# Cross attention's values by seven block products with sums made in DRAM, weight splits on VectorE alone, output products by heads, in a one-core fp32 decoder layer

## The chip, the cores and the metric

The kernel runs on one core of a Trainium2 chip. The metric is the time of one execution in device microseconds (us); a version is judged by the median of several runs. A profile records one more execution; its own time stands beside its span, since the span starts with the first recorded instruction. Engines in the rows: PE is TensorE, PEld its weight load, DVE is VectorE, ACT is ScalarE, POOL is GpSimd, SP is SyncE, which here only issues DMAs. A name with a q (SPq, POOLq) is the engine's sequencer.

## What is computed

One layer of a decoder in fp32, 256 tokens of width 1024, with 256 memory tokens. The part that the change touches is cross attention (4 heads of 256) and its surroundings:

```python
def memory_cross_attention(h, mem, wq, wkv, wo):
    q = (h @ wq).reshape(B, S, X_HEADS, X_HEAD_DIM)
    kv = mem @ wkv
    k = kv[..., :D_MODEL].reshape(B, M, X_HEADS, X_HEAD_DIM)
    v = kv[..., D_MODEL:].reshape(B, M, X_HEADS, X_HEAD_DIM)
    s = jnp.einsum('bshd,bmhd->bhsm', q, k).astype(jnp.float32) * (X_HEAD_DIM ** -0.5)
    p = jax.nn.softmax(s, axis=-1).astype(v.dtype)
    o = jnp.einsum('bhsm,bmhd->bshd', p, v).reshape(B, S, D_MODEL)
    return o @ wo
...
    h = h + merged @ w_out[l]
    h = h + memory_cross_attention(rmsnorm(h, norm_x_g[l]), rmsnorm(mem, norm_mem_g[l]),
                                   wq_x[l], wkv_x[l], wo_x[l])
    hn = rmsnorm(h, norm_ffn_g[l])
    gu = hn @ w_ffn_in[l]
    h = h + (jax.nn.silu(gu[..., :FFN_HIDDEN]) * gu[..., FFN_HIDDEN:]) @ w_ffn_out[l]
```

Ahead of it come an input projection, two token mixers (block attention and a gated recurrence) and their merge; behind it the FFN with 2816 hidden columns and a last norm.

## The kernel before

**Products in three parts.** Every fp32 operand is split into a high part, rounded to the format that TensorE takes at full rate (fp32r), and a low part, the rest. ScalarE makes the high part by a copy, another engine the low part by a subtraction. A product is three matmuls: high by high, high by low, low by high (`mm3`, `mm3t`, L261-269). `gemm_t` (L299) gives tokens on partitions: 48 matmuls of 128x512 for two groups of weights. `gemm_f` (L282) gives features on partitions: 32 matmuls (16 of 128x512, 16 of 128x256) for one group.

**Weights.** They come in units of 1 MB ([128, 2048] fp32) in the order of `plan` (L45). `prep` (L198) loads one on SyncE's queue into one of three raw buffers, and splits it in two halves of 1024 columns into one of three pairs of hi and lo buffers: ScalarE makes the high half (L223), and of the low half VectorE makes 576 columns and GpSimd 448 (`POOL_COLS`, L224-227), but for the first nine units, where VectorE makes all (`ALONE`). `nxt` (L234) hands out a unit and keeps two more prepared.

**Order.** The order of TensorE's instructions is written out by hand. A scheduler orders those of the other engines, but for some that are kept in program order. After each product of a unit, `tick` (L244) lets the background generators go one step.

**FFN with seven products.** Five pairs of FFN units already use a block scheme: 2 x 2 blocks of tokens and of weights are multiplied with seven products of 12 matmuls in place of eight, from sums of blocks (P1 to P7, `SEVEN`; `token_sums` L1287, `tokens` L1305, `product` L1312). The sums of weight blocks P5, P6, P7 (and a P4) are made in DRAM by `block_sums` (L746) as a background generator: for each group SyncE copies a block (L759, L760, L763), and GpSimd issues DMAs that add another (L748). Groups start every `SPACING` = 9 steps.

**Cross attention.** `memory` (L955) splits the memory times its norm's gain into `M2`. Four `gemm_f` make the keys, a `gemm_t` half of the values (`vx`, L1058), four `gemm_f` the queries with `scores` behind each, and a second `gemm_t` (L1094) the other half of the values. `ev_vx` scales an accumulator by the memory's norm and splits it into `vxh` and `vxl`. Then `pv` (L1099) runs for the four heads: 24 matmuls `xo` (128x256) from the probabilities `pp` and the values, and a split into `ox`. The four output units are prepared (L1113-1120), two of them in buffers of their own (`hix`, `lox`). The loop at L1223 makes the output for each token half t and column half c with 24 matmuls (`pso`) in both halves of k; `add_h2` (L1195) adds it to `H` and sums squares (`hjunk`), `rstd_h2` (L1200) takes `v`, then `r` by a power on GpSimd, then scales into `hn`; `turn_h2` (L1211) transposes (`h2T`) and makes `h2g` and the split `H2`, which is the FFN's left operand. FFN units are split by `halve` (L1136) in the order 0, 4, 1, 2, 3 first (`FIRST`).

Of the kernel before, what the change touches and what calls it, by code (L numbers as in the profile page):

```python
# [22 lines left out]
XH, XD = 4, 256  # L23
# [5 lines left out]
POOL_COLS = 896  # L29
ALONE = range(9)  # L30
# [41 lines left out]
SEVEN = ("P1", "P2", "P6", "P7", "P5", "P3", "P4")  # L72

# [22 lines left out]
SPACING = 9  # L96
# [50 lines left out]
def build(tc, A, out):  # L147
    nc = tc.nc
    V, SC, G, PE, SY = nc.vector, nc.scalar, nc.gpsimd, nc.tensor, nc.sync
    with ExitStack() as ctx:  # L150
# [46 lines left out]

        def prep(tags=None, raw=None):  # L198
            i = made[0]
            made[0] += 1  # L200
            first = i < 2
            if raw is None:
                raw = wr.tile([128, 2048], F32, name="raw", tag="raw")
            if tags is None:
                hi = wh.tile([128, 2048], F32R, name="hi", tag="hi")
                lo = wl.tile([128, 2048], F32R, name="lo", tag="lo")
            else:
# [8 lines left out]
            if sent == 1:  # L216
                SY.dma_start(raw, A["w"][i])
            for c in range(pieces):
                a = slice(c * n, (c + 1) * n)
                if i == 0:  # L220
                    SY.dma_start(raw[:, a], piece(A["w"][i], a))
                    yield
                SC.activation(hi[:, a], raw[:, a], AF.Copy)  # L223
                cut = (c + 1) * n - (0 if i in ALONE else POOL_COLS // pieces)  # L224
                for eng, b in ((V, slice(c * n, cut)), (G, slice(cut, (c + 1) * n))):
                    if b.start < b.stop:
                        eng.tensor_tensor(lo[:, b], raw[:, b], hi[:, b].bitcast(F32), op=ALU.subtract)  # L227
            ready[i] = (hi, lo)
# [5 lines left out]
        def nxt(lead=LEAD):  # L234
            i = at[0]
            at[0] += 1
            while made[0] <= min(i + lead, len(ORDER) - 1):
                run(prep())
            return ready.pop(i)
# [13 lines left out]
        def start(g):  # L253
            bg.append(g)
# [57 lines left out]
        def split(src, hi, lo, scale=None):  # L312
            if scale is None:
                SC.activation(hi, src, AF.Copy)
                V.tensor_tensor(lo, src, hi.bitcast(F32), op=ALU.subtract)  # L315
            else:
                SC.activation(hi, src, AF.Copy, scale=scale)
                V.scalar_tensor_tensor(lo, src, scale, hi.bitcast(F32), op0=ALU.mult, op1=ALU.subtract)
# [423 lines left out]
        def block(q, name):  # L742
            i, kh = {"11": (1, 0), "21": (1, 1), "12": (0, 0), "22": (0, 1)}[name]
            return A["w"][where["I", q + i, kh]]

        def block_sums():  # L746
# [8 lines left out]
            for g, q in enumerate(DOUBLES):  # L755
                t1, t2_, t3 = (dr.tile([128, 2048], F32, name="%s_%d" % (z, q)) for z in ("t1", "t2", "t3"))
                scr[q] = {"P5": t1, "P6": t2_, "P7": t3}
                i = SPACING * g
                at_step(i, lambda t=t3, q=q: tc.keep_in_program_order(SY.dma_start(t, block(q, "22"))))  # L759
                at_step(i + 6, lambda t=t1, q=q: tc.keep_in_program_order(SY.dma_start(t, block(q, "11"))))  # L760
                at_step(i + 4, lambda t=t3, q=q: add(t, q, "12"))
                at_step(i + 10, lambda t=t1, q=q: add(t, q, "12"))
                at_step(i + 8, lambda t=t2_, t3=t3: tc.keep_in_program_order(SY.dma_start(t, t3)))  # L763
                at_step(i + 12, lambda t=t2_, q=q: add(t, q, "11"))
                if g == 0:
                    t4 = dr.tile([128, 2048], F32, name="t4")
                    scr[q]["P4"] = t4
                    at_step(i + 16, lambda t=t4, t2_=t2_: tc.keep_in_program_order(SY.dma_start(t, t2_)))
                    at_step(i + 20, lambda t=t4, q=q: add(t, q, "21"))
# [184 lines left out]

        def memory():  # L955
# [3 lines left out]
            for k in range(8):  # L959
                split(raw[:, k], Mh[:, k], Ml[:, k], gv[:, V_MEM + k:V_MEM + k + 1])  # L960
# [11 lines left out]
        mg = memory()  # L972
        start(mg)
# [55 lines left out]
        drain(mg)  # L1029
# [19 lines left out]
        pp = big("P2", "pp", (128, 2, 4, 2, 256), F32R)  # L1049
        ph, pl = pp[:, 0], pp[:, 1]  # L1050

        def ev_vx(c):
            def ev(t, ps):
                a = slice(c * 512, (c + 1) * 512)
                split(ps, vxh[:, t, a], vxl[:, t, a], mem["r"][:, t:t + 1])
            return ev

        gemm_t((Mh, Ml), ev_vx(0))  # L1058
        drain(h1g)

# [36 lines left out]
        oxh, oxl = ox[:, 0], ox[:, 1]  # L1097

        def pv(x):  # L1099
# [5 lines left out]
            split(po, oxh[:, 2 * x:2 * x + 2], oxl[:, 2 * x:2 * x + 2])  # L1105

        for x in range(XH):
            for g in sg[:x + 2]:
                drain(g)
            pv(x)  # L1110
# [5 lines left out]
        for tags in (("B10", "B11"), ("B12", "B6")):  # L1116
            if made[0] < i0 + 4:
                run(prep(tags))
        wo = [by_k(ready.pop(i0 + i), 4) for i in range(4)]
        at[0] += 4  # L1120
# [7 lines left out]
        drain(bs)  # L1128
# [7 lines left out]
        def halve(raw, n):  # L1136
# [12 lines left out]
            for c in range(2):  # L1149
                a = slice(c * 1024, (c + 1) * 1024)  # L1150
                pin(SC.activation(hi[:, a], raw[:, a], AF.Copy))  # L1151
            pieces = 2 if n < 2 else 1
            w = 2048 // pieces
            for c in range(pieces):
                a = slice(c * w, (c + 1) * w)
                pin(V.tensor_tensor(lo[:, a], raw[:, a], hi[:, a].bitcast(F32), op=ALU.subtract))  # L1156
# [30 lines left out]
        def wo_part(ps, t, c, kh):  # L1187
            t_part(ps, wo[2 * c + kh], (oxh, oxl), t, kh)

# [3 lines left out]
        h2g = {}  # L1193
# [6 lines left out]
        def rstd_h2(t):  # L1200
            V.tensor_scalar(v2[:, t:t + 1], ssq2[:, 2 * t:2 * t + 1], ssq2[:, 2 * t + 1:2 * t + 2], EPS,
                            op0=ALU.add, op1=ALU.add)
# [21 lines left out]
        for t in range(2):  # L1224
            for c in range(2):
                ps = mm.tile([128, 512], F32, name="pso", tag="mm")
# [60 lines left out]
        def token_sums():  # L1287
            a11, a12, a21, a22 = (h2g[t, c] for t in range(2) for c in range(2))

            def put(i, g):  # L1290
                SC.activation(SS[:, 0, i], g, AF.Copy)
                V.tensor_tensor(SS[:, 1, i], g, SS[:, 0, i].bitcast(F32), op=ALU.subtract)

# [3 lines left out]
            put(1, s2)  # L1297
            yield
            V.tensor_tensor(a21, a11, a21, op=ALU.subtract)
            put(2, a21)  # L1300
            put(0, a22)
            V.scalar_tensor_tensor(a12, s2, -1.0, a12, op0=ALU.mult, op1=ALU.subtract)
            put(3, a12)

        def tokens(name):  # L1305
            if name in ("P1", "P2", "P4"):
                t, kh = {"P1": (0, 0), "P2": (0, 1), "P4": (1, 1)}[name]
                return [[z[:, 4 * kh + k, t * 128:(t + 1) * 128] for k in range(4)] for z in X2]
            i = {"P5": 0, "P6": 1, "P7": 2, "P3": 3}[name]
            return [[SS[:, z, i, k] for k in range(4)] for z in range(2)]  # L1310

        def product(ps, name, w, first):  # L1312
            xh, xl = tokens(name)
            for k in range(4):
                for i, (x, z) in enumerate(((xh, w[0]), (xh, w[1]), (xl, w[0]))):
                    PE.matmul(ps, x[k], z[:, k], start=first and k == 0 and i == 0, stop=k == 3 and i == 2,  # L1316
                              skip_group_check=not first)
# [16 lines left out]
        def ffn_product(n):  # L1334
# [7 lines left out]
            product(ps, name, w, first)  # L1342
# [168 lines left out]
```

## Time and profile before

| | |
|---|---|
| median of 3 runs | 613.69 us (613.41 to 613.7) |
| profiled execution, its own time | 613.31 us |
| its span | 611.5 us |
| TensorE busy | 602.4 us |
| VectorE busy | 456.2 us |
| ScalarE busy | 372.4 us |
| GpSimd busy | 271.0 us |

The profile's page has the busy times, a chain of what ended last, groups of instructions by line and the DMA queues. A row of the timeline gives the start, the duration, engine, line, operation, output and inputs, size, and in brackets the idle time before it and what ended that. A row of the waits gives the engine, the tile and line of what waited, what it waited for, and the total, the number and the longest. A row of a window gives for each engine in turn the busy time and number of instructions, then TensorE's granted clock, the share of the DMA engines and GB/s. Cross attention lies between some 303 and 437 us.

### The profile page before, as it was taken

What the parts mean: (1) busy time and instruction counts of PE and PEld (TensorE: products, weight loads), DVE (VectorE), ACT (ScalarE), POOL (GpSimd) and SP (SyncE); (2) the same over time, 40 slices, a digit from 0 to 9 for tenths busy, and PEclk for the clock granted to TensorE, in tenths of its full rate; (3) what the DMA queues carried; (4) which work ended last, traced back from release to release, by engine and by line L of the source; (5) the groups of instructions that cost most, each with busy time, mean ns of one, the idle gap of its engine ahead of it and who ended that gap; (6) DMA issues with size and microseconds to landing.
All of it is one profiled execution on the core that took longest, in us unless ns stands there. A gap on an engine that the chain in (4) does not pass through costs nothing.

```text
span 611.5 us, 8497 instructions
## 1 busy us (share of the span) xinstructions
PE 602.4 (99%) x3093; PEld 502.8 (82%) x3093; DVE 456.2 (75%) x702; ACT 372.4 (61%) x603; POOL 271.0 (44%) x247
## 2 busy tenths in 40 slices
PE   8999999999999999999999999999999999999995
PEld 7888888888887887778888888888878888888884
DVE  7599988979856886647956655693896887878953
ACT  7695545333377666646546646684776767677732
POOL 3897943566545664455876877650000000000003
PEclk9999999999999999999999999999999999999998
DMA  9973588469767985689989968762849979797601
GB/s 346 356 296 139 186 265 343 170 206 335 231 281 213 318 275 206 208 249 309 349 270 300 275 275 244 235 246 106 345 164 333 369 267 388 236 380 223 248 2 69
DMA packets 21866, 156.81 MB, mean 256 GB/s; under 512 B 2752, under 2 KB 3392, under 8 KB 5312
## 3 DMA queue, kind: packets, MB, share of 16 engines
q1 hardware_dynamic: 18224, 134.46, 56.3%
q0 software_dynamic: 2880, 20.97, 17.5%
q10 hardware_dynamic: 720, 0.84, 0.4%
q8 instruction: 24, 0.39, 0.3%
q14 instruction: 18, 0.15, 0.1%
HBM read 155.21 MB, written 34.60 MB: 310 GB/s over the span
## 4 chain that ended last, share of the span: by engine, by line
PE 92%; DVE 4%; ACT 2%; issue 1%; POOL 0%; POOLq 0%; DVEq 0%; ACTq 0%
PE pst L267 13%; PE pst L268 13%; PE pst L269 13%; PE pqA L1316 8%; PE psf L288 7%; PE pqF L1316 4%; PE psf L289 4%; PE acc L269 3%; PE acc L267 3%; PE acc L268 3%; PE pqB L1316 2%; PE lp L642 2%; PE psg L543 1%; PE pso L269 1%; PE pso L268 1%; PE pso L267 1%
## 5 line engine op out<-in xcount | busy, mean ns | idle before, releaser
L227 POOL TENSOR_TENSOR lo<-raw,hi 128x448 fp32r<-128x448 f32 x106 | 159.7, 1522 | 98.5 <-ACT hi L223 96.6
L223 ACT ACTIVATE hi<-raw 128x1024 fp32r<-128x1024 f32 (+1 forms) x128 | 128.8, 1029 | 86.3 <-issue 39.1
L227 DVE TENSOR_TENSOR lo<-raw,hi 128x576 fp32r<-128x576 f32 (+2 forms) x128 | 134.6, 1059 | 53.4 <-ACT hi L223 52.3
L267 PE MATMUL pst<-hi,XX 128*128 128x512 f32 x224 | 90.4, 403 | 0.0
L269 PE MATMUL pst<-hi,XX 128*128 128x512 f32 x224 | 87.4, 390 | 0.0
L268 PE MATMUL pst<-lo,XX 128*128 128x512 f32 x224 | 87.3, 390 | 0.0
L1185 POOL DMA_DIRECT2D b<-t x4 | 3.6, 891 | 124.5 <-DVE fu L1249 124.5
L269 PEld LDWEIGHTS pst<-hi,XX 128*128 128x128 f32 x224 | 42.1, 188 | 9.0
L267 PEld LDWEIGHTS pst<-hi,XX 128*128 128x128 f32 x224 | 42.1, 188 | 8.8 <-issue 0.7
L268 PEld LDWEIGHTS pst<-lo,XX 128*128 128x128 f32 x224 | 42.1, 188 | 7.9
L1156 DVE TENSOR_TENSOR lo<-raw,hi 128x2048 fp32r<-128x2048 f32 (+1 forms) x18 | 36.8, 2050 | 10.6 <-ACT hi L1151 10.5
L1151 ACT ACTIVATE hi<-raw 128x1024 fp32r<-128x1024 f32 x32 | 32.0, 1051 | 7.4 <-PE acc L269 5.3
L1156 DVE TENSOR_TENSOR lo<-rawx,hi 128x2048 fp32r<-128x2048 f32 x12 | 27.4, 2287 | 8.8 <-ACT hi L1151 8.8
L1151 ACT ACTIVATE hi<-rawx 128x1024 fp32r<-128x1024 f32 x24 | 24.2, 1052 | 6.6 <-PE acc L269 2.7
L1316 PE MATMUL pqA<-hi,SS 128*128 128x512 f32 x80 | 26.4, 390 | 0.0
L269 PE MATMUL acc<-hi,hids 128*128 128x512 f32 x62 | 24.3, 392 | 0.7 <-DVE hids L315 0.7
L267 PE MATMUL acc<-hi,hids 128*128 128x512 f32 x62 | 24.5, 394 | 0.0
L268 PE MATMUL acc<-lo,hids 128*128 128x512 f32 x62 | 24.1, 389 | 0.0
L288 PE MATMUL psf<-H,hi 128*128 128x512 f32 x64 | 22.7, 398 | 0.0
L288 PE MATMUL psf<-M,hi 128*128 128x512 f32 x64 | 22.5, 394 | 0.0
L288 PE MATMUL psf<-XX,hi 128*128 128x512 f32 x64 | 22.4, 394 | 0.0
L1429 POOL TENSOR_TENSOR hg<-H,gf 128x512 f32<-128x512 f32 x3 | 3.9, 1287 | 38.7 <-DVE H L1421 38.6
(420 smaller groups left out, 1568.6 us busy)
## 6 DMA issues: line engine op xcount, KB each, us to landing
raw<-w SPq DMA_DIRECT2D x75, 1024.0 KB, 6.5
t<-w POOLq DMA_DIRECT2D x16, 1024.0 KB, 10.0
raw<-t SPq DMA_DIRECT2D x12, 1024.0 KB, 6.7
rawx<-w SPq DMA_DIRECT2D x10, 1024.0 KB, 7.7
rawx<-t SPq DMA_DIRECT2D x4, 1024.0 KB, 8.6
b<-w SPq DMA_DIRECT2D x4, 1024.0 KB, 9.3
b<-t POOLq DMA_DIRECT2D x4, 1024.0 KB, 8.7
raw<-w SPq DMA_DIRECT2D x4, 512.0 KB, 6.1
```

The costliest lines, as they stand in the source:

```text
L223: SC.activation(hi[:, a], raw[:, a], AF.Copy)
L227: eng.tensor_tensor(lo[:, b], raw[:, b], hi[:, b].bitcast(F32), op=ALU.subtract)
L267: PE.matmul(ps, xh, h, start=first, stop=False)
L268: PE.matmul(ps, xh, l, start=False, stop=False)
L269: PE.matmul(ps, xl, h, start=False, stop=last)
L288: PE.matmul(ps, w[0][:, k, a], X2[:, :, k], start=k == 0, stop=False)
L289: PE.matmul(ps[:, 0], w[1][:, k, a], X2[:, 0, k], start=False, stop=k == 7)
L543: PE.matmul(pss[c][t], z[:, k, t * 128:(t + 1) * 128], ws[c][0][:, k], start=z is Xh and k == 0, stop=False)
L642: PE.matmul(ps[:, j], KS[:, a0 + j], QQ[:, a0 + j], start=True, stop=True)
L1151: pin(SC.activation(hi[:, a], raw[:, a], AF.Copy))
L1156: pin(V.tensor_tensor(lo[:, a], raw[:, a], hi[:, a].bitcast(F32), op=ALU.subtract))
L1316: PE.matmul(ps, x[k], z[:, k], start=first and k == 0 and i == 0, stop=k == 3 and i == 2, skip_group_check=not first)
```

## The change

It has three parts.

1. The values are made by seven block products of 12 matmuls (84 in place of 96). They are put among the keys' four products in the order `CROSS`: key unit 0, P1, P2, key unit 1, P6, P7, key unit 2, P5, key unit 3, P3, P4, then the four query units. `block_sums` makes the sums P5, P6 and P7 of the values' weights in DRAM as a first group "vx"; its groups now start every 7 steps, P4 of the FFN's first group earlier (`T4`), and the last group at written-out steps (`LATE`). P4's weights come from P2's raw block, kept in B12 (`b21`), to which GpSimd adds P6 by a DMA. The memory times its gain is kept (`mg`) and split from there; `mem_sums` makes the sums of memory blocks. Evictions copy some accumulators (`keep`) and add two (`whole`) before `ev_vx`.
2. VectorE makes the low half of every weight unit whole; GpSimd has no part in it.
3. The output weights come with the halves of k outermost, and the products of (0,0) and (0,1) run head by head between `pv` 2 and `pv` 3. `issue_after` puts the split of the fourth output unit behind the one of `pv` 2, that of the first FFN unit behind the one of `pv` 3, and a low half of FFN unit 3 behind the second `v`. The third and the fourth output unit have other buffers of their own.

```diff
-POOL_COLS = 896
-ALONE = range(9)
...
     order += [("F", "wkv_x", c * 256) for c in range(4)]
-    order += tgroup("wkv_x", 1024)[:2]
+    order += tgroup("wkv_x", 1024)
     order += [("F", "wq_x", c * 256) for c in range(4)]
-    order += tgroup("wkv_x", 1024)[2:]
-    order += tgroup("wo_x", 0)
+    order += [("T", "wo_x", c * 512, kh) for kh in range(2) for c in range(2)]
...
+CROSS = (0, "P1", "P2", 1, "P6", "P7", 2, "P5", 3, "P3", "P4", 4, 5, 6, 7)
...
-SPACING = 9
+SPACING = 7
+T4 = (14, 18)
+LATE = (41, 47, 50, 60, 53, 60)
...
                 SC.activation(hi[:, a], raw[:, a], AF.Copy)
-                cut = (c + 1) * n - (0 if i in ALONE else POOL_COLS // pieces)
-                for eng, b in ((V, slice(c * n, cut)), (G, slice(cut, (c + 1) * n))):
-                    if b.start < b.stop:
-                        eng.tensor_tensor(lo[:, b], raw[:, b], hi[:, b].bitcast(F32), op=ALU.subtract)
+                V.tensor_tensor(lo[:, a], raw[:, a], hi[:, a].bitcast(F32), op=ALU.subtract)
+            if STREAM[i] == "P2":
+                G.dma_start(raw, scr["vx"]["P6"], accum_op=ALU.add)
...
-            for g, q in enumerate(DOUBLES):
+            for g, q in enumerate(("vx",) + DOUBLES):
...
             for k in range(8):
-                split(raw[:, k], Mh[:, k], Ml[:, k], gv[:, V_MEM + k:V_MEM + k + 1])
+                SC.activation(mg[:, k], raw[:, k], AF.Copy, scale=gv[:, V_MEM + k:V_MEM + k + 1])
+                split(mg[:, k], Mh[:, k], Ml[:, k])
...
+        def mem_sums():
+            a11, a12, a21, a22 = (mg[:, 4 * c:4 * c + 4, t * 128:(t + 1) * 128] for t in range(2) for c in range(2))
+            V.tensor_tensor(a22, a22, a21, op=ALU.subtract)
+            V.tensor_tensor(a21, a11, a21, op=ALU.subtract)
+            yield 1
+            s2 = t2("s2", (128, 4, 128))
+            V.scalar_tensor_tensor(s2, a22, -1.0, a11, op0=ALU.mult, op1=ALU.subtract)
+            V.scalar_tensor_tensor(a12, s2, -1.0, a12, op0=ALU.mult, op1=ALU.subtract)
+            put(SSm, 1, s2)
+            yield 1
+            put(SSm, 2, a21)
+            put(SSm, 0, a22)
+            yield 1
+            put(SSm, 3, a12)
...
-        for c in range(4):
-            gemm_f(M2, ev_sum(kxh, kxl, c))
...
-        gemm_t((Mh, Ml), ev_vx(0))
-        drain(h1g)
+        def cross_product(name):
+            if name == "P6":
+                drain(ms)
+            key = {"P1": "A", "P6": "A", "P5": "A", "P3": "A", "P2": "B", "P7": "F", "P4": "F"}[name]
+            first = name in ("P1", "P2", "P7")
+            if first:
+                bank_of[key] = mm.tile([128, 512], F32, name="pq" + key, tag="mm")
+            ps = bank_of[key]
+            product(ps, block_tokens((Mh, Ml), SSm, name), by_k(nxt(), 4), first)
...
-        for c in range(4):
-            gemm_f(H1, ev_sum(qxh, qxl, c))
-            g = scores(c)
+        for u in CROSS:
+            if u in SEVEN:
+                cross_product(u)
+                continue
+            if u < 4:
+                gemm_f(M2, ev_sum(kxh, kxl, u))
+                continue
...
-        gemm_t((Mh, Ml), ev_vx(1))
...
+        pv(0)
+        pv(1)
...
+        run(prep(("P0",)))
...
+        wo_part(0, 0, 0)
+        wo_part(0, 0, 1)
+        pv(2)
+        wo_part(0, 1, 0)
+        wo_part(0, 1, 1)
+        drain(sg[3])
+        with tc.issue_after(turned_v[2]):
+            run(prep(("B12", "B6")))
+        wo.append(by_k(ready.pop(i0 + 3), 4))
+        wo_part(0, 0, 2)
+        pv(3)
+        drain(bs)
+        wo_part(0, 1, 2)
...
         for t in range(2):
             for c in range(2):
...
-                for kh in range(2):
-                    wo_part(ps, t, c, kh)
-                add_h2(t, c, ps)
+                for x in range(0 if t else 3, 4):
+                    wo_part(t, c, x)
+                add_h2(t, c, pso[t, c])
```

More of the change, by code (lines that the diff above doesn't have):

```diff
@@ L72, with stream @@
 SEVEN = ("P1", "P2", "P6", "P7", "P5", "P3", "P4")
+CROSS = (0, "P1", "P2", 1, "P6", "P7", 2, "P5", 3, "P3", "P4", 4, 5, 6, 7)
+def stream():
+    n = next(n for n, u in enumerate(ORDER) if u[0] == "I")
+    k = [ORDER.index(("F", w, c * 256)) for w in ("wkv_x", "wq_x") for c in range(4)]
+    return list(range(k[0])) + [k[u] if isinstance(u, int) else u for u in CROSS] + list(range(k[7] + 1, n))
+STREAM = stream()
 def ffn_plan():
@@ L1150, in halve @@
                 a = slice(c * 1024, (c + 1) * 1024)
-                pin(SC.activation(hi[:, a], raw[:, a], AF.Copy))
+                with tc.issue_after(turned_v[3]) if n == 0 else nullcontext():
+                    pin(SC.activation(hi[:, a], raw[:, a], AF.Copy))
             pieces = 2 if n < 2 else 1
@@ L1155, in halve @@
                 a = slice(c * w, (c + 1) * w)
-                pin(V.tensor_tensor(lo[:, a], raw[:, a], hi[:, a].bitcast(F32), op=ALU.subtract))
+                with tc.issue_after(behind[n]) if n in behind else nullcontext():
+                    pin(V.tensor_tensor(lo[:, a], raw[:, a], hi[:, a].bitcast(F32), op=ALU.subtract))
             return hi, lo
@@ L1192, in build @@
         r2 = cp.tile([128, 2], F32, name="r2")
-        h2g = {}
+        h2g, behind = {}, {}
         def add_h2(t, c, ps):
@@ L1296, in token_sums @@
             V.scalar_tensor_tensor(s2, a22, -1.0, a11, op0=ALU.mult, op1=ALU.subtract)
-            put(1, s2)
+            put(SS, 1, s2)
             yield
             V.tensor_tensor(a21, a11, a21, op=ALU.subtract)
-            put(2, a21)
-            put(0, a22)
+            put(SS, 2, a21)
+            put(SS, 0, a22)
             V.scalar_tensor_tensor(a12, s2, -1.0, a12, op0=ALU.mult, op1=ALU.subtract)
[L1303 to L1317, printed above, removed]
+            put(SS, 3, a12)
         bank_of, kept = {}, {}
```

154 lines of the change are left out of this document (106 added, 48 removed).

## Prediction

> **What bounds the kernel now.** I read the page's first lines and its chain first, then TensorE's waits, then its timeline in a quiet stretch and in the stage that changes.
>
> ```profile
> span 611.5 us, 8497 instructions
> ...
> PE 602.4 (99%) x3093; PEld 502.8 (82%) x3093; DVE 456.2 (75%) x702; ACT 372.4 (61%) x603; POOL 271.0 (44%) x247
> ...
> PE 92%; DVE 4%; ACT 2%; issue 1%; POOL 0%; POOLq 0%; DVEq 0%; ACTq 0%
> ```
> ```profile
> PE warm L364 <- DVE still L361: 1.6, 1, 1.6
> PE acc L269 <- DVE hids L315: 0.7, 1, 0.7
> PE xo L264 <- DVE vxl L318: 0.4, 1, 0.4
> ```
> ```profile
> 303.07 0.39 PE L267 MATMUL pst<-hi,mm 128*128 128x512 f32 x1
> ...
> 305.56 0.39 PE L269 MATMUL pst<-hi,mm 128*128 128x512 f32 x1
> ```
>
> The chain runs on TensorE for 92% of the span, and TensorE waits three times, 2.7 us in all. A busy share of 99% alone says little, since matmuls overlap: each 128x512 lasts 0.39 us. What counts is the distance of their starts: 11 steps in 2.49 us, **0.227 us** a step, no gap. So a removed matmul is worth its 0.227 us, but any wait that the change puts into this stream is paid in full, for almost no slack absorbs it.
>
> The Trainium skill (Perfetto Trace Analysis, Identifying the Most-Contended Engine) says that matmul busy time is a bad measure and that the busy share of weight loads is a good one. By it, 82% would leave TensorE room, and an order that feeds it better could win several per cent; the unbroken starts above disagree, and I go by them.
>
> **The change, part by part.** All times are on the profiled execution's clock, whose own time is 613.31 us (span 611.5 and 1.8 around it); the median of the three runs, 613.69, lies 0.38 above, and I add that at the end.
>
> *1. Values by block products.* Two `gemm_t` calls of 48 matmuls become seven products of 12, so 96 become 84: 12 x 0.227 = **-2.7 us**, certain as long as nothing waits.
>
> ```profile
> 405.63 0.28 PE L262 MATMUL xo<-pp,vxh 128*128 128x256 f32 x1
> 405.75 0.28 PE L263 MATMUL xo<-pp,vxh 128*128 128x256 f32 x1
> 406.46 0.39 PE L264 MATMUL xo<-pp,vxl 128*128 128x256 f32 x1 [0.44 <-DVE vxl L318]
> ```
>
> The value product no longer runs last ahead of `pv`, so the last eviction is done long before; this gap is 0.71 against a pitch of 0.12: **-0.6 us**.
>
> The products need sums of weights (DMA), sums of memory tokens (VectorE, ScalarE) and evictions. I cost them at nothing while each is ready before its use.
>
> ```profile
> 327.00:370.00 43.00, 43.00 (x237) 37.25 (x236) 25.68 (x36) 26.16 (x45) 31.64 (x26) 1.00 0.84 282
> 370.00:409.00 39.00, 38.56 (x242) 34.55 (x241) 27.25 (x60) 27.30 (x52) 28.58 (x23) 1.00 0.74 231
> ```
>
> In 327 to 409 us TensorE (second column) is full; VectorE has 29 us free of 82, and the DMA share is 0.84 and 0.74. The memory sums add 5 VectorE sums, 4 lo halves and some 5 combining steps, about 0.7 us each by the 128x512 rows below: some 10 us, which fits into the 29. The cover is thinnest where a unit's weights are prepared one product earlier than used; that is the second rival.
>
> *2. Splits on VectorE alone.*
>
> ```profile
> L227 DVE TENSOR_TENSOR lo<-raw,hi x128: 684/760/3131, 5.0 to 397.3; 128x576 fp32r<-128x576 f32 x106, 128x1024 fp32r<-128x1024 f32 x14, 128x512 fp32r<-128x512 f32 x8
> ...
> L227 POOL TENSOR_TENSOR lo<-raw,hi x106: 1131/1665/1757, 53.2 to 397.7; 128x448 fp32r<-128x448 f32 x106
> ```
> ```profile
> 406.33 0.67 DVE L315 TENSOR_TENSOR pp<-xT,pp 128x512 fp32r<-128x512 f32 x1
> 406.93 1.21 DVE L1156 TENSOR_TENSOR lo<-raw,hi 128x1024 fp32r<-128x1024 f32 x1
> ```
>
> A half took VectorE 0.76 us (up to 3.13 beside GpSimd) while GpSimd needed 1.67; now VectorE needs 1.21. So a half is ready 0.46 us sooner where both started together, VectorE is held 0.45 longer, or up to 1.9 shorter where it was held up. Bounds for 106 halves: VectorE +48 us of work against 155 us idle, or less work than before. On TensorE I take **0**: no split ended a wait of it in the list above.
>
> *3. Output products by heads.* Before, all of `pv` was done ahead of the first `pso`. Now `pv` 2 and 3 and the products of heads 0 to 3 alternate, and each piece has less cover:
>
> ```profile
> 414.10 0.39 PE L269 MATMUL pso<-hi,ox 128*128 128x512 f32 x1
> ```
> ```profile
> 404.63 0.58 ACT L314 ACTIVATE pp<-xT 128x512 fp32r<-128x512 f32 x1
> ...
> 408.91 1.07 ACT L1151 ACTIVATE hix<-raw 128x1024 fp32r<-128x1024 f32 x1 [0.35 <-PE xo L263]
> 409.88 0.57 ACT L314 ACTIVATE ox<-xo 128x512 fp32r<-128x512 f32 x1
> ...
> 422.34 1.34 ACT L1207 ACTIVATE hn<-H,r 128x512 f32<-128x512 f32 x2 [0.93 <-POOL r L1203]
> ```
> ```profile
> 414.52 0.69 DVE L1197 TENSOR_TENSOR H<-pso,H 128x512 f32<-128x512 f32 x1 [0.65 <-PE pso L269]
> 419.96 0.69 DVE L1197 TENSOR_TENSOR H<-pso,H 128x512 f32<-128x512 f32 x1 [4.75 <-PE pso L269]
> 421.44 0.21 DVE L1201 TENSOR_SCALAR v<-ssq 128x1 f32<-128x1 f32 x1 [0.79 <-ACT hjunk L1198]
> ```
>
> A matmul group hands over 0.2 us after its last pitch ends (414.10 + 0.23 to 414.52); I use 0.25. Then ScalarE's hi 0.58 and VectorE's lo 0.67: **1.5 us** at least from the transpose or `pv` to the product that reads its low half. Against that:
> - `pv` 1 reads the low half of head 1's probabilities 13 `xo` matmuls after their transpose, 13 x 0.12 = 1.56; VectorE has a short step of another head's softmax ahead, which makes the 1.5 some 1.85: **+0.3**.
> - `pv` 3 reads head 3's after 6 products, 6 x 0.227 = 1.36: **+0.2**. Bounds of these two: 0, and 1.2 more (a 1.21 split ahead on VectorE).
> - Head 3's product has the same 1.36 of cover, and the low half is its third matmul, so 1.81. ScalarE's program has a hi half of an FFN unit (its buffer waits for the same `pv` 3) ahead of head 3's `ox`: from 408.91 to 409.88 that held it 0.97. 0.25 + 0.97 + 0.57 + 0.67 = 2.46, less 1.81: **+0.7**. Bounds 0 (no such half ahead) and 1.9 (a 1.21 split as well).
> - (0,0) and (0,1) now both end only 24 matmuls, 5.45 us, ahead of the transposes of token half 0. Before, (0,1) took 4.0 from its end (0.24 ahead of 419.96) to the end of `hn` (423.68) over `H`, square, `v`, `r` (GpSimd) and `hn`; 1.5 are left, and VectorE's program has two 1.21 splits and a 2.28 one among these: **+0.4**. Bounds 0, and 3.2 (all three ahead).
>
> Sum: +1.6.
>
> *4. Start of the FFN.* `issue_after` and the later release of the output weights' buffers move the FFN units' splits.
>
> ```profile
> 428.73 2.28 DVE L1156 TENSOR_TENSOR lo<-raw,hi 128x2048 fp32r<-128x2048 f32 x1
> ...
> 432.13 0.68 DVE L1197 TENSOR_TENSOR H<-pso,H 128x512 f32<-128x512 f32 x1
> ...
> 440.89 1.28 DVE L1218 TENSOR_TENSOR h2g<-h2T,gv 128x512 f32<-128x512 f32 x2
> 442.28 1.30 DVE L1220 TENSOR_TENSOR H<-h2g,H 128x512 fp32r<-128x512 f32 x2
> ```
> ```profile
> 431.57 0.39 PE L1316 MATMUL pqA<-hi,H 128*128 128x512 f32 x1
> ...
> 443.34 0.39 PE L267 MATMUL psi<-hi,H 128*128 128x512 f32 x1
> ...
> 458.76 0.50 PE L269 MATMUL acc<-hi,hids 128*128 128x512 f32 x1 [0.72 <-DVE hids L315]
> ```
>
> Call E the end of the last `pso` (431.57). Unit 2's 2.28 us split lay 2.8 us ahead of E. By heads, each weight group serves both token halves to the last, and the buffer that unit 2 takes comes free only 12 matmuls (2.7 us) ahead of E; two hi halves (2.0) must follow, so the split lies at E - 0.4 to E + 1.8. The last `H` (E + 0.56 before) stands behind it: +1.2 us for `H`, `v`, `hn` and, as VectorE goes on in this order, for `h2g` and the low half of `H` (442.28). The product that reads that follows at 443.34, and TensorE already waits for `hids` at 458.76. So of the 1.2, some 0.5 is paid at the first place and the rest at the second: **+1.2**. Bounds: 0 (the split is short of E after all) and 2.2 (a whole split more).
>
> **Sum:** -2.7 - 0.6 + 1.6 + 1.2 = -0.5: profiled 612.8, **613.2** as a median. Own range: with the waits of parts 3 and 4 at half their size, 611.8; with the one that is least certain, that of the transposes, 2 us above its value, 615.2.
>
> **Rivals.**
>
> *A: the new waits are covered.* Each wait of part 3 is a difference of two numbers above 1 us, by a timeline that is laid out by hand. If part 3 costs nothing: -3.3 + 1.2 = -2.1, **611.6**; if part 4 is nothing too, -3.3, **610.4**. For it: before has just one wait there (`xo`). Against it: covers of 1.36 us stand against 1.5 us of work that can't be shortened.
>
> *B: key unit 2's weights land late, and the kernel is slower.*
>
> ```profile
> raw<-w SPq DMA_DIRECT2D x75, 1024.0 KB, 6.5
> t<-w POOLq DMA_DIRECT2D x16, 1024.0 KB, 10.0
> ```
> ```profile
> DMA to landing us min/median/max: 4.7/6.7/12.1
> ```
>
> Between key units 1 and 2 stand only two products (2 x 2.7 us). Unit 2's load starts when unit 1's split is read, about 3.5 us after key unit 0 ends; unit 2 is used 16.5 us after that end (four products of 2.73 and a key unit of 16 x 0.227 + 16 x 0.12 = 5.6). With 3.5 us for its split and 1 for what is queued, it must land within **8.5 us**. Weight loads in 280 to 400 us took 6.7, at most 12.1 (last row); an accumulate took 10.0, and one is now added at this very place (P6 onto P2's block), beside FFN sums that come closer together. At 10.0 the wait is 1.5 us, at 12.1 it is 3.6: 614.7 to 616.8, slower from a landing of 10.2 on; I price it at **615.8**. For it: SP and GpSimd both load here at a share of 0.84. Against it: 6.7 is the median under that share.
>
> The Trainium skill (DMA: Bandwidth & Descriptors, Queues, rings and completion order) says that each DMA engine goes round between queues packet by packet; by it a load beside the accumulate keeps at least half the rate, and twice its 6.7 us, an estimate, would be past 8.5. Before's 12.1 fits that; no run yet shows this pair.
>
> *C: the splits on VectorE alone make it late* somewhere in 41 to 320 us, where nothing else changes: four halves of 0.45 us queued in a row would be 1.8, about **615**. *D: the change doesn't take the matmuls away:* excluded, TensorE's program has 12 fewer.
>
> **How the numbers follow.** Forecast 0.40, A 0.35, B 0.20, C 0.05. Measurement tells 0.2% (1.2 us) from no change, so "same" is 612.5 to 614.9: the forecast. A is faster, B and C slower: 0.35, 0.40, 0.25. The likeliest case's own range is 611.8 to 615.2, nearly all of it in "same". For 8 in 10 I reach to the near part of A (610.7) and of B (615.5).
>
> **What would show it.** 12 fewer matmuls and no `vxl` wait: step 1. TensorE's waits listed for low halves of `pp` and `ox`, about 1.2 us together, one for `hn` or the `h2T` transposes: step 3; none of them: A. `H` of (1,1) over 1 us behind E and longer waits for `H` and `hids`: step 4. A wait for key unit 2's split, with its load over 8.5 us: B. Waits before 320 us: C. It would be wrong altogether if block sums for the FFN came too late behind the denser copies (SP's waits for accumulates), far behind this stage.

## The result and the profile after

The changed kernel took **627.12 us** (626.41 to 630.06) beside 613.70 for the kernel before on the same chip: 1.0232 times as long (95% interval 1.0215 to 1.025), 13.4 us slower. The forecast was 613.2. The profiled execution of the changed kernel took 626.41 us with a span of 624.5.

The page's first lines, after:

```profile
span 624.5 us, 8352 instructions
...
PE 604.8 (97%) x3081; PEld 501.0 (80%) x3081; DVE 465.0 (74%) x720; ACT 384.3 (62%) x624; POOL 119.2 (19%) x141
```

TensorE has 12 matmuls fewer, as it should, and yet is busy 2.4 us longer; GpSimd's busy time has fallen from 271.0 to 119.2 us. What TensorE waited for (engine, tile and line; then total us, times, longest):

```profile
PE mT L955 <- POOL tat L950: 4.9, 2, 3.3
PE warm L389 <- DVE still L386: 1.6, 1, 1.6
PE psf L315 <- DVE lo L251: 1.5, 1, 1.5
PE acc L295 <- DVE hids L340: 1.3, 1, 1.3
PE h2T L1346 <- ACT hn L1337: 1.3, 1, 1.3
PE pst L294 <- DVE lo L251: 0.8, 1, 0.8
PE pst L293 <- ACT hi L250: 0.6, 1, 0.6
PE xs L295 <- POOL qxl L1111: 0.5, 1, 0.5
PE xo L289 <- DVE pp L340: 0.5, 1, 0.5
```

Eleven waits in ten rows (the smallest, 0.2, isn't shown) in place of three. To weigh them I set the starts of the same matmuls of both traces beside each other. Up to 285 us the two agree within 0.3 us. From there to 309 us the changed kernel falls **8.3 us** behind, before cross attention has begun. From the first key product to the first query product it loses 2.0, among the query products 0.7, and from the first `pv` to the end 6.7, of which some 2.2 are 20 matmuls of scores and transposes that now run behind that `pv`: 4.5 on balance. The matmuls saved give 2.7 back, and 12.9 are left at the last matmul.

**Where the 8.3 us come from.** First the stretch from 227 to 257 us (columns: PE, PEld, DVE, ACT, POOL busy, clock, DMA share, GB/s), before, then after:

```profile
227.00:257.00 30.00, 29.99 (x169) 23.53 (x168) 19.89 (x66) 20.29 (x47) 11.57 (x9) 1.00 0.52 183
```
```profile
227.00:257.00 30.00, 29.99 (x169) 23.54 (x168) 20.50 (x65) 19.63 (x47) 6.25 (x8) 1.00 0.95 273
```

TensorE does the same work in both, but the DMA share goes from 0.52 to 0.95. The DMAs issued in that stretch (number, size, median us to landing), before:

```profile
raw<-w SPq DMA_DIRECT2D x4, 1024.0 KB, 4.8
mraw<-mT SPq DMA_DIRECT2D x1, 1024.0 KB, 4.8
```

And after, with the DMA engines' time by queue (packets, MB, share; software is GpSimd's accumulates, hardware SyncE's loads and copies), what SyncE's queue waited for, and when the memory's load landed:

```profile
q0 software_dynamic: 476, 3.51, 57.1%
q1 hardware_dynamic: 407, 4.65, 37.8%
...
t<-w POOLq DMA_DIRECT2D x6, 1024.0 KB, 24.2
raw<-w SPq DMA_DIRECT2D x4, 1024.0 KB, 16.0
```
```profile
SPq L789 <- DMA t<-w: 12.0, 1, 12.0
```
```profile
DMA to landing us min/median/max: 23.6/23.6/23.6
```

Before, GpSimd issued no accumulating DMA in that stretch, weights landed in 4.8 us and the memory (`mraw`) in 4.8. After, it issued six:

```profile
227.39 0.92 POOL L773 DMA_DIRECT2D t<-w  x1
231.33 1.72 POOL L773 DMA_DIRECT2D t<-w  x2
236.86 0.81 POOL L773 DMA_DIRECT2D t<-w  x1 [3.81 <-issue]
246.24 0.83 POOL L773 DMA_DIRECT2D t<-w  x1 [8.57 <-issue]
256.42 0.82 POOL L773 DMA_DIRECT2D t<-w  x1 [9.35 <-issue]
```

They landed one after another, at 236.6, 245.9, 256.1, 265.8, 273.2 and 280.7, so at most three were under way at once, and the last three took 24 to 29 us each. A copy (`t2`) that must wait for one of them stands 12.0 us at the head of SyncE's queue, and the weights and the memory behind it can't be issued. Yet the memory is issued only 1.8 us later than before; most of its delay is the landing. The issue before, then after:

```profile
255.50 0.33 SPq L949 DMA_DIRECT2D mraw<-mT  x1
```
```profile
257.27 0.43 SPq L975 DMA_DIRECT2D mraw<-mT  x1
```

What follows on ScalarE, TensorE and in a window:

```profile
280.87 1.31 ACT L988 ACTIVATE mg<-mraw,gv 128x256 f32<-128x256 f32 x3 [5.13 <-DMA mraw<-mT]
...
285.25 1.99 ACT L250 ACTIVATE hi<-raw 128x1024 fp32r<-128x1024 f32 x2
```
```profile
301.88 0.66 PE L955 MATMUL mT<-cst,tat 128*128 128x128 f32 x4 [3.32 <-POOL tat L950]
304.08 1.12 PE L955 MATMUL mT<-cst,tat 128*128 128x128 f32 x4 [1.55 <-POOL tat L950]
304.85 0.78 PE L293 MATMUL pst<-hi,oah 128*128 128x512 f32 x1
305.43 0.63 PE L294 MATMUL pst<-lo,oah 128*128 128x512 f32 x1
305.85 0.63 PE L295 MATMUL pst<-hi,oal 128*128 128x512 f32 x1
306.28 0.63 PE L293 MATMUL pst<-hi,oah 128*128 128x512 f32 x1
```
```profile
304.80:307.40 2.60, 2.60 (x9) 2.13 (x8) 2.60 (x5) 1.55 (x2) 0.00 (x0) 0.61 0.59 104
```

ScalarE stands 5.13 us for the memory (first row), and when the next weight unit lands at 283.1 it has the memory's work still to do and splits the unit only from 285.25. Then the memory's splits and sums, the late weights' splits and the merge (`tat`) fall together. TensorE waits 3.3 and 1.6 us for `tat`, and after such a wait its matmuls start 0.43 us apart, not 0.227, for 2 us: the last row shows a granted clock of 0.61. That is part of why it is "busy" longer for less work: of the 8.3 us lost here, waits make 6.3. The Trainium skill (TensorE: Matmul & The Clock Gate, "Wait — 56ns, not 53.3ns?") gives 426.7 ns between starts of 512 columns at the cold clock; these rows agree with it.

### The profile page after: what moved, and what is told of

Read it like the earlier page. It is cut to its first block, busy times and chain, and to the rows that moved or that the text cites. A ratio compares the mean times of both kernels' runs of the same rounds, so it can differ in the third digit from the quotient of the medians.

```text
span 624.5 us, 8352 instructions
## 1 busy us (share of the span) xinstructions
PE 604.8 (97%) x3081; PEld 501.0 (80%) x3081; DVE 465.0 (74%) x720; ACT 384.3 (62%) x624; POOL 119.2 (19%) x141
## 4 chain that ended last, share of the span: by engine, by line
PE 72%; DVE 9%; DMA 9%; issue 4%; ACT 4%; POOL 1%; POOLq 0%; DVEq 0%; ACTq 0%; SPq 0%
PE pst L293 10%; PE pst L294 10%; PE pst L295 10%; PE pqA L1077 7%; DMA raw<-w 5%; PE pqF L1077 4%; DMA mraw<-mT 4%; PE acc L295 3%; PE acc L293 3%; PE acc L294 3%; PE psf L314 3%; DVE lo L251 3%; PE pqB L1077 2%; PE lp L667 2%; PE psf L315 1%
## 5 line engine op out<-in xcount | busy, mean ns | idle before, releaser
L251 DVE TENSOR_TENSOR lo<-raw,hi 128x1024 fp32r<-128x1024 f32 (+1 forms) x130 | 160.5, 1249 | 43.7 <-ACT hi L250 43.2
L250 ACT ACTIVATE hi<-raw 128x1024 fp32r<-128x1024 f32 (+1 forms) x130 | 130.2, 1028 | 94.6 <-PE pst L295 68.4
L1287 DVE TENSOR_TENSOR lo<-raw,hi 128x2048 fp32r<-128x2048 f32 (+1 forms) x18 | 36.9, 2052 | 10.3 <-ACT hi L1281 10.2
L294 PE MATMUL acc<-lo,hids 128*128 128x512 f32 x62 | 24.2, 390 | 0.0
L1287 DVE TENSOR_TENSOR lo<-b,hi 128x2048 fp32r<-128x2048 f32 x7 | 16.0, 2291 | 7.2 <-ACT hi L1281 7.2
L315 PE MATMUL psf<-M,lo 128*128 128x256 f32 x64 | 18.2, 284 | 1.5 <-DVE lo L251 1.5
```

The lines of the kernel that those rows point to most:

```text
L294: PE.matmul(ps, xh, l, start=False, stop=False)
L315: PE.matmul(ps[:, 0], w[1][:, k, a], X2[:, 0, k], start=False, stop=k == 7)
```

## The experiments

All against the kernel before on the same chip; times in us. The theories are numbered as they came.

**1. One part at a time.**

`splits_alone`, on the kernel before:
```diff
-POOL_COLS = 896
+POOL_COLS = 0
```


> The kernel before with one edit: VectorE makes the low half of every weight unit, GpSimd none. Theory 1 (GpSimd's queue was paced by its splits; without them its accumulating DMAs run ahead of their plan, pile up and delay loads): some accumulates are issued 10 to 30 us earlier than before (before: 259.15, 273.11, 279.63), the memory's load takes over 8 us (before 4.8), and the time rises, by 1 to 5 us, less than with the changed kernel since there are three copies and three accumulates fewer. Theory 2 (VectorE has too much to do with 128x1024 splits): accumulates stay at their places, VectorE is busy without gaps near 285 to 308 us, and TensorE waits for low halves: 2 to 6 us. My prediction: no change (613.7 within 1.2).

612.81 against 613.84: 0.9977 (0.9963 to 0.9992), a little faster. VectorE alone is enough for the splits, so theory 2 fails here. The accumulates do come earlier, as theory 1 says (228.80, 232.76 and 246.14 in place of 259.15, 273.11 and 279.63), but the memory's load landed in 6.1 and the time didn't rise: the pace alone makes no pile that TensorE feels.

`after_gpsimd_splits`, on the changed kernel: the four lines of the old split (`cut`, two engines) put back.

> The changed kernel with the splits divided between VectorE and GpSimd as before, the other two parts kept. Both theories take the wait at 285 to 309 us (8.3 us) to come from this part: 618 to 620 us in place of 627.1. Theory 1 adds that the memory's load lands within 10 us in place of 23.6 and the accumulates between 227 and 257 us are spread out. If the time stays above 625 us, the added sums (three copies and three accumulates more, groups every 7 steps) are the cause and not the splits.

632.8, 1.0296 (1.0272 to 1.032). The division of the splits doesn't cause the loss; taking it back costs 5.7 more.

`after_paced`, on the changed kernel:
```diff
                 V.tensor_tensor(lo[:, a], raw[:, a], hi[:, a].bitcast(F32), op=ALU.subtract)
+                if i > 8:
+                    G.tensor_tensor(pace, raw[:, a][:, 0:16], hi[:, a][:, 0:16].bitcast(F32), op=ALU.subtract)
```


> The changed kernel, with a GpSimd subtraction of 128x16 from each half of a weight unit (its result isn't used): GpSimd waits for each split as before, and VectorE's work is unchanged. Theory 1: the accumulates come at the pace of the units again, the memory's load lands within 10 us, the wait at 285 to 309 us falls from 8.3 to under 3: about 620 us. Theory 2: nothing changes there, 626 to 628 us.

626.52, 1.0193 (1.0167 to 1.0219), runs from 623.3 to 630.0. Theory 1 fails in what it promised: the memory landed in 13.4 in place of 23.6 and the wait at 285 to 309 us went, but SyncE then stood 11.0 us for an accumulate at 293 to 304 us, and TensorE waited 3.0 at 316.7 for what came of it, with 6.7 us at a granted clock of 0.50 behind. The pile had moved, not gone. (The profiled execution is the slowest of the five.)

`after_heads_undone`, on the changed kernel: `pv` for all heads first, `wo` by halves of k, no `issue_after`.

> The changed kernel with the third part undone: all of the probability-by-value products first, the output products by halves of k, the FFN's first splits as before. The first two parts are kept. By the trace of the changed kernel the third part's waits are 0.6 (pp), 0.5 (ox), 1.5 (h2T), 0.5 (psi) and 0.6 more at hids, 3.7 in all: 623.4 us. By the prediction's sum, 2.8: 624.3. The rival is that this part pays for something (the values' earlier place leaves the last head's softmax without cover): then 626 or more.

627.0, 1.0203 (1.0177 to 1.023): no change. The third part's waits go, but `pv` now waits for the last heads' probabilities (1.8 us), which the second values product used to cover.

**2. Which DMAs.** Theory 3 replaced pacing: the sums' DMAs themselves.

`after_plain_blocks`, on the changed kernel: no sums for the values, the FFN's sums at the steps of the kernel before:
```diff
-SPACING = 7
-T4 = (14, 18)
+SPACING = 9
+T4 = (16, 20)
...
-            return scr["vx"][u] if u in scr["vx"] else block("vx", names[u])
+            return block("vx", dict(names, P5="12", P6="11", P7="22")[u])
...
-            if STREAM[i] == "P2":
-                G.dma_start(raw, scr["vx"]["P6"], accum_op=ALU.add)
...
-            for g, q in enumerate(("vx",) + DOUBLES):
+            for g, q in enumerate(DOUBLES):
...
-                at = LATE if q == DOUBLES[-1] else [i + n for n in (0, 4, 6, 10, 8, 12)]
+                at = [i + n for n in (0, 4, 6, 10, 8, 12)]
```


> The changed kernel without the sums of the values' weights: the seven products read plain blocks of the weights, no copies and accumulates are made for them, and the FFN's sums keep the steps of the kernel before (every 9). So the values are not those of the reference; matmuls, memory sums, evictions, splits and the order by heads are all kept. Theory 3, formed after the last four runs (pacing fell): the added sums' DMAs make accumulates slow, SyncE's queue waits in order for one of them (12.0 us at 244 to 256 us), and the weights and the memory queued behind come late. Then the wait at 285 to 309 us (8.3) and the one at key unit 2 (2.1) go: 616 to 618 us. Theory 2 (the memory's and the splits' work on VectorE and ScalarE is too much by itself): over 622 us.

626.9, 1.0227 (1.0206 to 1.0248), 9 to 11 us above what was expected. The wait at 285 to 309 us is gone whole, with all of the memory's new work in place (its load landed in 6.5), which refutes theory 2 there. But the key stage took 48.2 us where it needs 42.6, nearly all of it lost at 358 to 365, and the queries' stage 6.1 more than without waits. SyncE's waits from 330 to 352 us, and its next issues:

```profile
SPq L244 <- DVE lo L251: 12.1, 1, 12.1
SPq L787 <- DMA t<-w: 10.5, 1, 10.5
```
```profile
348.31 0.48 SPq L787 DMA_DIRECT2D t<-t  x1
348.96 1.72 SPq L244 DMA_DIRECT2D raw<-w  x3
```
```profile
358.72 0.50 PE L1075 MATMUL pqA<-hi,SSm 128*128 128x512 f32 x1 [2.76 <-ACT hi L250]
```

With the old steps an FFN copy now stands in the key stage, 10.5 us, and three weight loads go out together behind it. The kernel before has such waits too (9.6 at most) and hides them; here TensorE uses a block unit up in 12 x 0.227 = 2.7 us, not 5.5, so a lead of two units covers about half as long (this reason is argued; no run changes the lead). Among the queries ScalarE stood 6.99 us for a weight unit that took 11.4 us beside two of the FFN's accumulates, with the queries' splits behind it.

`after_t2_later`, on the changed kernel:
```diff
-T4 = (14, 18)
+T4 = (19, 23)
...
-                at = LATE if q == DOUBLES[-1] else [i + n for n in (0, 4, 6, 10, 8, 12)]
+                at = LATE if q == DOUBLES[-1] else [i + n for n in (0, 4, 6, 10, 11, 15)]
```


> The changed kernel with the steps of the sums moved: the copy that waits for an accumulate is issued 7 steps after it in place of 4, and the accumulate behind that copy 3 steps later. The same DMAs, the same work. Theory 3: SyncE's waits for accumulates (25.6 us in 3) shrink, and with them the wait at 285 to 309 us, to under 4 us: 621 to 624 us, if nothing piles up elsewhere. Theory 2: 626 to 628.

628.86, 1.0255 (1.0239 to 1.0271). SyncE's waits for accumulates fell to 7.3, and the memory was issued as early as in the kernel before:

```profile
255.30 0.33 SPq L975 DMA_DIRECT2D mraw<-mT  x1
```

It still took 23.6. The waits near 286 us are gone, but 6.6 us were lost at 300 to 306 (and 6.4 more among the queries). So the head of SyncE's queue is not the only way: a row of accumulates delays a load that is issued on time, and by this run that is the larger part of the 8.3 us.

**3. Amount or place.**

`after_no_sums`: as `after_plain_blocks`, with plain blocks for the FFN too and no `block_sums`, so it leaves out every sum of weights made in DRAM. `after_vx_sums_only`: on the changed kernel, the values' sums kept and the FFN's left out:
```diff
-            for g, q in enumerate(("vx",) + DOUBLES):
+            for g, q in enumerate(("vx",)):
```


> The changed kernel without any sum of weights made in DRAM, the values' and the FFN's: the products read plain blocks, so values and FFN are not the reference's. Matmuls, memory sums, splits and weight loads are kept. Theory 3 (the sums' copies and accumulates delay the weight loads, by load on the DMA engines and by SyncE waiting in its queue for an accumulate ahead of the weights): no wait at 285 to 309 us, the stage from the first key product to the first query product falls from 44.6 us (48.2 with plain blocks) to 41.5 to 42.5, the time is 613 to 615 us; what is left over is the third part. Theory 4 (the three raw buffers are too few for units that TensorE uses up in 2.7 us in place of 5.5, with or without sums): that stage stays at 44 us or more, 617 us or more.

> The changed kernel with the values' sums alone; the FFN's five groups aren't made and the FFN reads plain blocks, so it is not the reference's. Theory 3: the values' sums by themselves, early and few, cost nothing: as without any sums, within 1.5 us (613 to 616), with the accumulate onto P2's block as the one DMA left in the key stage. If they cost over 3 us, the accumulate onto P2's block is a cause by itself.

614.79, 1.0017 (1.0005 to 1.0028), and 614.97, 1.0016 (1.0004 to 1.0028). Key stage 42.6 us in both, no lost time in it. So some 12 us of the 13.4 belong to the sums' DMAs, and the values' own sums, with the accumulate onto P2's block, cost nothing by themselves. Theory 4 fails: three raw buffers do for the short units.

`plain_t2_later`: `after_plain_blocks` with copies 3 steps later, as above.

> As with plain blocks (no sums for the values, FFN sums every 9 steps), and each copy that waits for an accumulate 3 steps later, as the accumulate behind it. With plain blocks SyncE stood from 338 to 348 us for an accumulate of the FFN's, ten us, with three weight loads behind, and TensorE waited 6.5 us at 358 to 365. Theory 3: that wait goes; from the first key to the first query product 42 to 44 us in place of 48.2, the time 621 to 624 us in place of 626.9. Theory 4: 47 to 49 us, 626 to 628.

620.99, 1.0108 (1.0061 to 1.0155), but between 616.5 and 623.6; in the profiled one the key stage took 42.6. With these steps the time differs from run to run by 7 us.

`sums_moved`, on the changed kernel: every DMA kept, only steps changed:
```diff
-SPACING = 7
-T4 = (14, 18)
-LATE = (41, 47, 50, 60, 53, 60)
+SPACING = 9
+T4 = (16, 20)
+LATE = (48, 52, 54, 60, 58, 60)
+VX = (1, 6, 11, 16, 14, 25)
...
-                i = SPACING * g
+                i = SPACING * (g - 1)
-                at = LATE if q == DOUBLES[-1] else [i + n for n in (0, 4, 6, 10, 8, 12)]
+                at = LATE if q == DOUBLES[-1] else VX if q == "vx" else [i + n for n in (0, 4, 6, 10, 8, 12)]
```


> The changed kernel with the same sums at other steps: the FFN's first four groups every 9 steps as in the kernel before, the values' six DMAs between them (steps 1, 6, 11, 16, 14, 25), the FFN's last group only after the key products (48, 52, 54, 60, 58, 60). Same DMAs, same work. Theory 3 (it is when the sums' DMAs run, not how many there are or what the other engines do): the memory's load lands within 10 us, the wait at 285 to 309 us (8.3) is under 2, the key stage takes 42.6 to 43.5 us, the time 615 to 617, near the 614.97 without the FFN's sums. If the DMAs' sheer amount is the cause: 620 us or more.

**614.54**, 1.0004 (0.9989 to 1.0018): as without the FFN's sums. It is the place of the DMAs, not their amount. Its memory landed in 10.2. The first key and the first query product, in the changed kernel and then here:

```profile
335.55 0.48 PE L314 MATMUL psf<-M,hi 128*128 128x512 f32 x1
...
380.11 0.39 PE L314 MATMUL psf<-H,hi 128*128 128x512 f32 x1
```
```profile
327.12 0.48 PE L315 MATMUL psf<-M,hi 128*128 128x512 f32 x1
...
369.71 0.39 PE L315 MATMUL psf<-H,hi 128*128 128x512 f32 x1
```

The key stage starts 8.4 us earlier and takes 42.6 in place of 44.6.

**4. The end of cross attention.** In the changed kernel VectorE, GpSimd and TensorE at the last `hn`:

```profile
441.38 0.39 PE L1077 MATMUL pqA<-hi,H 128*128 128x512 f32 x1
```
```profile
443.11 0.69 DVE L1325 TENSOR_TENSOR H<-pso,H 128x512 f32<-128x512 f32 x1
444.65 0.21 DVE L1329 TENSOR_SCALAR v<-ssq 128x1 f32<-128x1 f32 x1 [0.85 <-ACT hjunk L1326]
444.78 2.28 DVE L1287 TENSOR_TENSOR px<-raw,px 128x2048 fp32r<-128x2048 f32 x1
```
```profile
444.94 2.54 POOL L1333 TENSOR_TENSOR r<-v,nhalf 128x1 f32<-128x1 f32 x1 [11.42 <-DVE v L1329]
```
```profile
448.29 1.27 PE L1346 MATMUL h2T<-cst,hn 128*128 128x128 f32 x8 [1.30 <-ACT hn L1337]
```

The power for the norm, one column, takes 2.54 us: VectorE's subtraction started 0.16 us ahead of it and ends at 447.06, and the power ends just behind, at 447.48. Before, it took 0.55. `issue_after` has put that subtraction right behind `v`.

`after_px_behind_r` (on the changed kernel), `heads_px_behind_r` (on `splits_and_heads`) and `sums_moved_px` (on `sums_moved`) have one edit:
```diff
-            if t:
-                behind[3] = v.ins
             G.tensor_tensor(r2[:, t:t + 1], v2[:, t:t + 1], nhalf[:, :1], op=ALU.pow)
+            if t:
+                behind[3] = V.tensor_scalar(v2[:, t:t + 1], r2[:, t:t + 1], 1.0, None, op0=ALU.mult).ins
```


> The changed kernel, with the low half of FFN unit 3 (128x2048 on VectorE) held back until GpSimd's power is done, by a 128x1 step on VectorE that reads its result. In the changed kernel the power took 2.54 us beside that subtraction, 0.57 without one. Theory: the power waits for VectorE's subtraction to end; here it takes under 0.7 us, the wait for h2T (1.5) goes, and the time falls by 1.5 to 2.5 us. Rival: the transposes wait for something else (the square, the scaling) and the time stays within 0.5 us.

The power after that edit:

```profile
447.56 0.56 POOL L1331 TENSOR_TENSOR r<-v,nhalf 128x1 f32<-128x1 f32 x1 [11.42 <-DVE v L1329]
```

The power takes 0.56, the wait for `hn` is gone, and from the first FFN product to the last matmul it is 174.3 us in place of 176.3. The time, 626.7 (1.0214, 1.0197 to 1.0232), hardly shows it: in the profiled execution the first key product comes 1.3 us later than in the changed kernel and the key stage takes 46.8 us in place of 44.6.

`splits_and_heads`: the kernel before with the second and third part, no other.

> The kernel before with the second and the third part (splits on VectorE alone, output products by heads), the values by two plain products as before. The second part alone gave 0.9977 of before, 1.4 us less. My prediction's sum for the third part: +2.8 less the 0.6 that isn't to be had here, so 615 to 616 us. If the third part costs nothing without the first (taking it back from the changed kernel gave 627.0 in place of 627.1), 612.8.

> The kernel before with the second and the third part and the power freed (617.08 without the last, 612.81 with the second part alone). The power took 2.53 us beside the 128x2048 subtraction. Expected: 0.57 us, no wait at h2T, from the first FFN product to the end 2.0 us shorter as in the changed kernel (176.3 to 174.3): 615 us. If the third part's cost lies elsewhere: 616.5 or more.

617.08, 1.0066 (1.0049 to 1.0084), and 615.14, 1.0034 (1.0012 to 1.0055). Against `splits_alone` (612.81, 0.9977) the third part on its own costs 4.3 by the medians and 5.5 by the ratios, and 2.0 of that is the power.

> As sums_moved, with the power freed from the 128x2048 subtraction beside it, which took 2.0 us off the FFN stage in two kernels. Theory: 2.0 us under sums_moved, 613 to 615 us. It is also the best version of the change that the runs point to; the second part alone gave 612.81.

> As sums_moved, with the third part undone in place of the power freed (the power then isn't beside that subtraction). The matmuls saved (-2.7) and the splits (-1.4) remain; the last heads' softmax has lost the cover of the second values product, which cost 1.8 us in the changed kernel without the third part. So 613.7 - 2.7 - 0.6 - 1.4 + 1.8 and what the sums still cost (0 to 2): 611 to 613 us. If the third part pays for itself here, this is no faster than sums_moved_px.

`sums_moved_px`: **612.61**, 0.9971 (0.996 to 0.9983), a little faster than the kernel before and 14.5 us faster than the changed one. It isn't distinguishable from `splits_alone` (0.9963 to 0.9992), which has the second part only: the first and the third part together, repaired, gain nothing that these runs show. TensorE's waits in it:

```profile
PE warm L390 <- DVE still L387: 1.6, 1, 1.6
PE acc L296 <- DVE hids L341: 1.3, 1, 1.3
```

`moved_px_heads_undone` (`sums_moved` without the third part): 613.73, 0.9996 (0.9981 to 1.001), 0.7 us above what was expected: without the by-heads order `pv` loses 1.8 waiting for probabilities, and `pqA` 0.9. Once its power is free, the third part earns its place beside the first.

## Why the prediction was wrong, point by point

- **"I cost them at nothing while each is ready before its use"** (step 1) is what failed. I looked at 327 to 409 us, where the sums are used, and at VectorE's free time there. They are made from 41 us on, on queues that other loads share. With all sums taken out, with the FFN's taken out, or with all of them moved the time is 614.5 to 615.0, so this term was about **12 us**, not 0. The last sentence of the prediction did name sums made too late, but for the FFN and behind this stage; most of the harm came ahead of it, to the memory and the merge.
- **-2.7 for 12 matmuls** was right, as far as a sum can show: the whole change with its sums moved and the power freed takes 1.55 us off the kernel before; matmuls (-2.7), splits (-1.0) and a third part with its power freed (615.14 against 612.81, +2.3) add up to -1.4. These are medians; by the ratios it is -0.6 against -1.8, so the two agree to about 1 us.
- **-0.6 for the `vxl` wait:** that wait is gone, as forecast.
- **Splits at 0:** -1.0 us alone by the medians, -1.4 by the ratio (interval -2.3 to -0.5), better than 0. On the changed kernel they were worth 5.7. How they help is argued only: GpSimd needed 1.67 us a half against VectorE's 1.21.
- **Rival B** had the right place and mechanism for a small part: key unit 2's load was issued at 346.55, took 10.2 us beside the added accumulate and one of the FFN's, and TensorE lost 1.7 us there (1.5 had been priced at 10.0). Without the FFN's sums it lost nothing, so it was not the added accumulate alone.
- **Rival C** had the place, since TensorE waits ahead of 320 us, and the wrong cause: the splits alone made the kernel faster. It says that nothing else changes from 41 to 320 us; the sums' DMAs do, and that is the same slip as in step 1. **Rival A** fails too: the waits of part 3 were not covered.
- **The new waits, +1.6 by hand:** from the first `pv` to the first FFN product `splits_and_heads` takes 30.6 us, 2.1 more than `splits_alone`. Single items, in the changed kernel, were off: `pv` 1 0.6 (0.3 forecast), `pv` 3 nothing (0.2), head 3 0.4 (0.7), the first transposes 0.2 (0.4).
- **FFN start, +1.2:** `H` came 1.73 us behind the end of the last `pso` (0.56 before), a delay of 1.2 as worked out, and with the power freed the FFN stage is 1.1 longer than in `splits_alone` (174.2 against 173.1). Missing was the power beside a subtraction, 2.0 us more. The prediction named the moved split but not what it would run beside.
- **Only roughly settled:** how the 8.3 us divide between the copy at the head of SyncE's queue and the load on the DMA engines. Each was seen to do harm by itself (`after_plain_blocks`, `after_t2_later`). In `after_t2_later`, with that copy out of the way, 6.6 of them stayed; that is one profiled execution.

## What to carry to other kernels

Work that is moved onto DMA is costed where it is made, not only where it is used: list every DMA that it adds, with the queue that it stands in, what it waits for there, and which loads stand behind it. When a change makes TensorE use a weight unit up in half the time, a lead counted in units covers half the time as well, and waits that were hidden before can come out. A wait added to steer the order puts two instructions side by side: look at what they share.

## What the runs showed of the hardware

- Accumulating DMAs of 1 MB from DRAM to DRAM took 10.0 us to land in the kernel before and 24.2 when six were issued within 30 us (medians). Those six landed one after another, 7.4 to 10.2 us apart. In that stretch accumulates took 57.1% of the DMA engines' time for 3.51 MB, SyncE's loads and copies 37.8% for 4.65 MB: per MB twice as much.
- A GpSimd power of one column that met a VectorE subtraction of two SBUF operands ended just behind it: it took 2.54 us in place of 0.56. The Trainium skill (SBUF — State Buffer, Who interferes with whom) says that a VectorE instruction with two SBUF inputs contends with a GpSimd instruction that reads SBUF, over ports that one holds exclusively, and that the order of issue decides which one blocks; both rows agree.
- After a wait of 3.0 us TensorE's matmuls started 0.43 us apart for 6.7 us (`after_paced`), which cost as much again as the wait:

```profile
316.70:323.40 6.70, 6.50 (x14) 4.68 (x15) 3.70 (x5) 2.22 (x4) 1.05 (x2) 0.50 1.01 404
```
